# Seven products for the last feed-forward block's down-projection, the factors of gate and up exchanged, and the states' decay on GpSimd

## The chip, the cores and the metric

The kernel runs on one core of a Trainium2 chip. The metric is the device time of one execution in microseconds (us). Engines: TensorE does matmuls (PE in the profile; PEld is its weight load), VectorE (DVE) and ScalarE (ACT) work element by element and read PSUM, GpSimd (POOL) works element by element in SBUF and issues some transfers, SyncE (SP) issues the other transfers. Results of matmuls land in PSUM, eight banks of 128 x 512 fp32.

## The reference

Two layers of a streaming encoder, for 512 frames of a new stream and 8 x 16 frames of running streams: 640 rows of 1024 in all. A layer is a feed-forward block, a mixer, a feed-forward block; each is wrapped in a layer norm. So there are four feed-forward blocks, ffn0 to ffn3, of the form

```python
def swiglu(x, w_gate, w_up, w_down):
    return (jax.nn.silu(x @ w_gate) * (x @ w_up)) @ w_down
x = layer_norm(ALPHA * x + 0.5 * swiglu(x, w_gate, w_up, w_down), g, b)
```

with a hidden width of 2816 (22 rows of 128 in the kernel's layout). The first mixer is a state-space model beside stick-breaking attention, the second one a state-space mixer whose running states must be returned:

```python
h_new = h * jnp.exp(cs[:, -1])[..., None, None] + jnp.einsum('bsgr,bsgn,bsgrp->bgrpn', to_end, b_c, x_c)
```

For the 8 running streams the kernel does this last update (decay by el, plus one product) in ffn3's time, in 32 steps of 128 x 512.

## The kernel before, in words

**Precision.** All large products run in fp32r with both factors split into a high and a low part: `split` copies on ACT (the high part), then subtracts on DVE (the low part). A product is three matmuls: high x high, low x high, high x low. Weights come in as fp32 raw tiles of 128 x 1024 (four buffers, `raw`) through SP and are split into w tiles (`two_units`, six buffers) or a w1 tile (`unit`, one buffer).

**A feed-forward block.** The normed rows lie transposed as xhi and xlo (8 x 128 channels by 640 tokens). The hidden rows f = 0..21 are made in transposed form, 128 hidden channels by 640 tokens. Rows 0 and 1 and the gate of rows 2 and 3 are made with plain products (`mm3`). From row 2 on, rows are made in pairs (`pair`, f and f+1): one gate matrix and one up matrix, each a 2 x 2 block product done by seven products of blocks instead of eight (`matrix`, `product`): the weights are cut in two by hidden row and in two by input channel, x in two by channel and in two by token. Each of the seven is 12 matmuls of 320 columns. The sums of x blocks are built once per block, at the start of the stage, into the tiles T1, T2 and T4 and into x itself (`both`, earlier `minus`, and `t3_split`); the sums of weight blocks are built per matrix (`operands`) from two raw tiles. `take` is called when one of the four results is complete: for gate it applies silu, for up it multiplies by the gate, and after the last half of a hidden row `finish` splits the row into an h tile.

Four hidden rows at a time go through the down-projection, `down`, which adds into yacc (640 tokens by 1024 on five tiles of 128 tokens). It is placed between the gate and the up matrix of the next pair, so that the rows it needs are old. The last four rows (18 to 21) follow directly on the last up matrix, together with the layer norm. In the plain form it is, for each token tile t and half j, 12 matmuls of 512 columns (`tm_proj`). In the stages named in `SEVEN` the inner down-projections run as `down7`: token tile 4 stays plain, and token tiles 0 to 3 are done by seven products of blocks, with sums of hidden rows (`row_sums`, into an hs tile) and sums of weights (built in the raw tiles in place).

**PSUM.** Two pools of four banks, a and b. Gate and up use a, three banks per matrix; the plain down-projection uses b.

**Order.** The instructions of an engine are put in order by the compiler's scheduler, which takes what is ready by its own estimate, in the program's order of priority; `issue_after` adds an edge. Each engine then runs its list in order.

**The side work of ffn3.** `ssd_states` is a generator of 32 steps. `tick` advances it at given places: after a gate matrix, after an up matrix, and after token tiles 0, 2 and 4 of a down-projection. A step issues, on SP, the loads of the factors (twelve transfers every second step) and of the state; then one matmul (L1475), a multiplication by the decay (L1477, DVE), an addition of the matmul's result (L1478, DVE), and a transfer out (SP).

Lines that matter: L96 and L95 (the two halves of `split`), L141 (`mm3`), L218 (the sum into yacc in `tm_proj`), L345 (sums of weights), L366 (the matmuls of `product` in gate and up), L377 (`keep`, PSUM to SBUF on ACT), L403 and L411 (additions in gate and up), L415 and L418 (multiplications in up), L502 (the matmuls of `down7`), L510, L513 and L514 (its sums into yacc: DVE, or ACT and an accumulating transfer from POOL).

Of the kernel before, what the change touches and what calls it, by code (L numbers as in the profile page):

```python
# [9 lines left out]
F32 = mybir.dt.float32  # L10
# [11 lines left out]
T = 640  # L22
TP = 512
# [7 lines left out]
SEVEN = ("ffn1", "ffn2")  # L31
# [5 lines left out]
def kernel(ctx: ExitStack, tc: tile.TileContext, I, O, phases=PHASES):  # L37
# [28 lines left out]
    def bank_a():  # L66
        return bank("a")
# [10 lines left out]
    state = {"silu": None, "preload": None}  # L78
# [142 lines left out]
    def ffn(i, ph, last, side=None):  # L221
# [4 lines left out]
        with ExitStack() as st:  # L226
# [59 lines left out]
            g_row = lambda: wk.tile([128, T], F32, name="s", bufs=2)  # L286
            for r in range(2):
# [3 lines left out]
                for c in range(2):  # L291
                    p = bank_a()[:, :Q]
# [9 lines left out]
            def minus(t, p, m):  # L302

                u = wk.tile([128, T], F32, name="hf", bufs=2)[:, :Q]
                V.tensor_tensor(t, quad(hf32, *p)[:, k], quad(hf32, *m)[:, k], op=ALU.subtract)
                V.tensor_tensor(u, quad(lf32, *p)[:, k], quad(lf32, *m)[:, k], op=ALU.subtract)  # L306
                V.tensor_tensor(t, t, u, op=ALU.add)  # L307

            t2, t3 = (wk.tile([128, 4, Q], F32, name="h", bufs=4) for _ in range(2))
            for k in range(4):  # L310
                t1 = wk.tile([128, Q], F32, name="mx", bufs=3)
                minus(t3[:, k], (1, 1), (0, 1))
                minus(t1, (0, 1), (0, 0))
                for part in (hf32, lf32):
                    V.tensor_tensor(t2[:, k], t3[:, k] if part is hf32 else t2[:, k], quad(part, 0, 0)[:, k], op=ALU.add)  # L315
                split(tq[2][:, 0, k], tq[2][:, 1, k], t2[:, k])
                split(tq[1][:, 0, k], tq[1][:, 1, k], t1)
# [5 lines left out]
            for k in range(4):  # L323
# [3 lines left out]
            B = {1: (quad(xh, 0, 0), quad(xl, 0, 0)), 2: (quad(xh, 1, 0), quad(xl, 1, 0)),  # L327
                 3: (quad(xh, 1, 1), quad(xl, 1, 1)), 4: (tq[4][:, 0], tq[4][:, 1]), 5: (tq[1][:, 0], tq[1][:, 1]),
                 6: (tq[2][:, 0], tq[2][:, 1]), 7: (quad(xh, 0, 1), quad(xl, 0, 1))}

            def operands(src0, src1):
# [3 lines left out]
                a11, a12, a21, a22 = r0[:, :512], r0[:, 512:], r1[:, :512], r1[:, 512:]  # L335
                A = {}

                def part(w, src, *ps):
                    for n, p in enumerate(ps):
                        A[p] = w[:, n]  # L340
                    state["lo"] = split2(w, src).ins

                def total(o, v, w, op):
                    with tc.issue_after(state["lo"]):
                        V.tensor_tensor(o, v, w, op=op)  # L345
# [12 lines left out]
                A[4] = unit()  # L358
                split(A[4][:, 0], A[4][:, 1], a22)
                return A  # L360

            def product(ps, A, p, first):
                n = 0
                for k in range(4):
                    for a, b in ((0, 0), (1, 0), (0, 1)):
                        nc.tensor.matmul(ps, A[p][:, a, k * 128:k * 128 + 128], B[p][b][:, k, :],  # L366
# [3 lines left out]
            def matrix(A, take):  # L370

                x, w, z = (bank_a()[:, :Q] for _ in range(3))
                e = {}

                def keep(n, ps):
                    e[n] = wk.tile([128, Q], F32, name="mx", bufs=3)
# [1621 lines left out]
```

## Time and profile before

| | |
|---|---|
| three runs | 2546.13, 2548.44, 2544.92 us (median 2546.13) |
| profiled execution | span 2543.3 us from the first to the last instruction; no time beside the span is given for it |
| TensorE | busy 2504.3 us (98%), mean granted clock 0.997 |
| VectorE, ScalarE, GpSimd | busy 1992.5 us (78%), 1220.5 us (48%), 306.2 us (12%) |
| HBM | 259.56 MB read, 40.54 MB written |

The stages follow each other: ffn0 to about 448 us, the first mixer to 745, ffn1 to 1175, ffn2 to 1595, the second mixer to 2100, ffn3 to the end. The profile's groups give, per line and form of instruction, a count, the busy time, the mean length and the idle time before it with what ended it. In the timeline a number in brackets is such an idle time. The lengths of neighbouring rows of one engine overlap a little, and PE's far more (a matmul's row is longer than the distance to the next), so distances between starts are the better measure there.

### The profile page before, as it was taken

Reading aid. Unit: us, or ns where it says so; the run is one execution under the profiler, and the core shown is the slowest. Engines: PE = TensorE matmul, PEld = TensorE weight load, DVE = VectorE, ACT = ScalarE, POOL = GpSimd, SP = SyncE. Lnnn points to the kernel's source line nnn. Section 1 sums busy time; section 2 is a strip of 40 time slices with the busy share of each in tenths; the row PEclk is TensorE's granted clock in tenths of the full one; section 3 lists DMA queues with packets and bytes.
Section 4 is the critical chain, followed back from the end, with each engine's and each line's share of the span. In section 5 each row is a group of like instructions: output and inputs, shape, how many; then the busy total and the mean of one; then the engine's idle time right before and its main releaser. Section 6 shows DMA issues by size and latency. Waiting matters only on the chain. (4 is left out here: it accounts for less than half of the span.)

```text
span 2543.3 us, 40461 instructions
## 1 busy us (share of the span) xinstructions
PE 2504.3 (98%) x15599; PEld 2293.3 (90%) x15599; DVE 1992.5 (78%) x3437; ACT 1220.5 (48%) x2245; POOL 306.2 (12%) x432
## 2 busy tenths in 40 slices
PE   9999999999999999999999999999999999999998
PEld 9999999878789999999999999888989879999997
DVE  7788777666879888878888887777676689886768
ACT  4443444436744555553455554566565544443332
POOL 0000001210130000013000002211121151000001
PEclk9999999999999999999999999999999999999999
DMA  5322334443221433361244443456564722543442
GB/s 185 108 93 92 107 118 154 149 163 111 73 83 61 118 102 105 101 174 54 67 112 112 112 114 117 129 182 185 161 201 142 234 84 85 168 148 107 144 140 95
DMA packets 175217, 317.42 MB, mean 125 GB/s; under 512 B 20864, under 2 KB 92160, under 8 KB 174512
## 3 DMA queue, kind: packets, MB, share of 16 engines
q1 hardware_dynamic: 165200, 293.83, 36.1%
q0 software_dynamic: 9824, 21.01, 4.0%
q8 instruction: 122, 2.00, 0.3%
q14 instruction: 71, 0.58, 0.1%
HBM read 259.56 MB, written 40.54 MB: 118 GB/s over the span
## 5 line engine op out<-in xcount | busy, mean ns | idle before, releaser
L96 DVE TENSOR_TENSOR w<-raw,w 128x512 fp32r<-128x512 f32 (+2 forms) x569 | 501.2, 904 | 80.6 <-ACT w L95 79.1
L95 ACT CAST w<-raw 128x512 fp32r<-128x512 f32 (+1 forms) x569 | 425.1, 784 | 280.0 <-PE bank L141 96.7
L366 PE MATMUL bank<-xhi,w 128*128 128x320 f32 x2432 | 540.2, 309 | 0.7 <-ACT mx L377 0.5
L141 PE MATMUL bank<-xhi,w 128*128 128x256 f32 (+2 forms) x2272 | 497.7, 311 | 1.3 <-ACT xhi L205 1.0
L141 PE MATMUL bank<-w,h 128*128 128x512 f32 x1872 | 435.3, 391 | 0.4 <-DVE yacc L218 0.4
L366 PE MATMUL bank<-T,w 128*128 128x320 f32 x2736 | 426.2, 309 | 1.4 <-DVE hf L411 1.1
L141 PEld LDWEIGHTS bank<-w,h 128*128 128x128 f32 x1872 | 348.9, 188 | 73.5 <-DVE yacc L218 1.2
L366 PEld LDWEIGHTS bank<-xhi,w 128*128 128x128 f32 x2432 | 407.3, 188 | 4.8 <-ACT mx L377 1.5
L366 PEld LDWEIGHTS bank<-T,w 128*128 128x128 f32 x2736 | 406.5, 188 | 3.1 <-DVE hf L411 1.8
L141 PEld LDWEIGHTS bank<-xhi,w 128*128 128x128 f32 x2272 | 377.7, 188 | 10.8 <-issue 6.1
L366 PE MATMUL bank<-xlo,w 128*128 128x320 f32 x1216 | 375.0, 308 | 0.0
L141 PE MATMUL bank<-xlo,w 128*128 128x256 f32 (+2 forms) x1136 | 350.9, 309 | 2.6 <-DVE xlo L206 2.5
L366 PEld LDWEIGHTS bank<-xlo,w 128*128 128x128 f32 x1216 | 228.0, 188 | 0.3
L141 PEld LDWEIGHTS bank<-xlo,w 128*128 128x128 f32 x1136 | 213.9, 188 | 5.6 <-DVE xlo L206 2.8
L218 DVE SCALAR_TENSOR_TENSOR yacc<-bank,yacc 128x512 f32<-128x512 f32 x160 | 109.2, 686 | 75.3 <-PE bank L141 74.9
L377 ACT COPY mx<-bank 128x320 f32<-128x320 f32 x228 | 96.3, 423 | 138.3 <-PE bank L366 137.5
L96 DVE TENSOR_TENSOR w<-sw,w 128x1024 fp32r<-128x1024 f32 x76 | 93.0, 1224 | 52.5 <-ACT w L95 52.2
L95 ACT CAST w<-sw 128x1024 fp32r<-128x1024 f32 x76 | 79.9, 1051 | 97.2 <-DVE sw L345 96.1
L514 POOL DMA_DIRECT2D yacc<-ev x56 | 48.6, 900 | 644.5 <-ACT ev L513 589.4
L141 PE MATMUL bank<-w,og 128*128 128x512 f32 x432 | 103.7, 394 | 2.5 <-DVE og L96 1.8
L141 PEld LDWEIGHTS bank<-w,og 128*128 128x128 f32 x432 | 79.7, 188 | 19.5 <-DVE og L96 2.5
L405 ACT ACTIVATE s<-s 128x320 f32<-128x320 f32 x108 | 50.8, 470 | 82.8 <-DVE s L403 82.6
(434 smaller groups left out, 3503.8 us busy)
## 6 DMA issues: line engine op xcount, KB each, us to landing
raw<-in_w_gate_dram SPq DMA_DIRECT2D x88, 512.0 KB, 3.8
raw<-in_w_up_dram SPq DMA_DIRECT2D x88, 512.0 KB, 4.0
raw<-in_w_down_dram SPq DMA_DIRECT2D x88, 512.0 KB, 3.6
raw<-in_m_in_dram SPq DMA_DIRECT2D x52, 512.0 KB, 5.0
yacc<-ev POOLq DMA_DIRECT2D x56, 256.0 KB, 4.3
raw<-in_m_out_dram SPq DMA_DIRECT2D x24, 512.0 KB, 3.9
csb<-cs_d SPq DMA_DIRECT2D x20, 512.0 KB, 5.2
h<-in_ssd_h_dram SPq DMA_DIRECT2D x16, 512.0 KB, 6.1
```

The costliest lines, as they stand in the source:

```text
L95: nc.scalar.copy(hi, src)
L96: return nc.vector.tensor_tensor(lo, src, hi.bitcast(F32), op=ALU.subtract)
L141: state["pe"] = nc.tensor.matmul(ps, a, b, start=(k == 0), stop=(k == n - 1)).ins
L218: state["acc"] = nc.vector.scalar_tensor_tensor(ya, pb, scale, ya, op0=ALU.mult, op1=ALU.add).ins
L366: nc.tensor.matmul(ps, A[p][:, a, k * 128:k * 128 + 128], B[p][b][:, k, :], start=(first and n == 0), stop=(n == 11), skip_group_check=True)
L377: nc.scalar.copy(e[n], ps)
L405: state["silu"] = nc.scalar.activation(t, ps, AF.Silu).ins
L514: nc.gpsimd.dma_start(yacc[:, t, 512 * j:512 * j + 512], e, accum_op=ALU.add)
```

## The change

1. `SEVEN` also holds ffn3, so its four inner down-projections run as `down7`. In ffn3 the ticks after token tiles fall away for these; instead there are two in `down7`, after products 2 and 3, and the step's matmul uses a bank of pool a there.
2. In gate and up, x is the first factor of the block product and the weights the second. The order of the products is 1, 5, 6, 2, 7, 3, 4, in place of 1, 2, 6, 5, 7, 3, 4. Product 1 is copied by ACT to a second bank (z) and both copies are added to by further products; so two of the four results (up to now one) are complete in PSUM. The two z banks are a pool of their own, and the banks of a fall from four to two. The sums of the weights are built in place in the raw tiles, the sw tile goes, and the mx tile has two buffers instead of three. The last result is now the second half of row f, where before it was the second half of row f+1.
3. Tokens are taken in other halves in `down7` (tiles 0 and 1 against 2 and 3, instead of alternate tiles). One of the four row sums goes into the half of row f's h tile that is then not needed (`finish` leaves it out), so hs has 768 columns instead of 1024.
4. The multiplication by the decay in a state step goes from DVE to POOL.

The diff, cut to its core:

```diff
-SEVEN = ("ffn1", "ffn2")
+SEVEN = ("ffn1", "ffn2", "ffn3")
...
-        psum(banks[-1], f"main{len(banks)}", a=4, b=4)
+        psum(banks[-1], f"main{len(banks)}", a=2, z=2, b=4)
...
     def bank_a():
-        return bank("a")
+        if state["turn"] is None:
+            return bank("a")
+        state["turn"] += 1
+        return bank("az"[state["turn"] % 2])
...
+            sums = [bank("z")[:, :Q] for _ in range(2)]
+            state["turn"] = None
...
             for k in range(4):
-                t1 = wk.tile([128, Q], F32, name="mx", bufs=3)
-                minus(t3[:, k], (1, 1), (0, 1))
-                minus(t1, (0, 1), (0, 0))
+                t1 = wk.tile([128, Q], F32, name="mx", bufs=2)
+                both(t1, (0, 1), (1, 1), ALU.add)
+                both(t3[:, k], (0, 0), (0, 1), ALU.subtract)
...
             def operands(src0, src1):
-                u, v, w = (two_units() for _ in range(3))
-                sums = wk.tile([128, 1024], F32, name="sw", bufs=1)
-                s2, s1 = sums[:, :512], sums[:, 512:]
-                part(u, r0, 1, 2)
-                total(s1, a21, a22, ALU.add)
-                total(s2, s1, a11, ALU.subtract)
-                part(v, sums, 6, 5)
-                total(a12, a12, s2, ALU.subtract)
-                total(a11, a11, a21, ALU.subtract)
-                part(w, r0, 7, 3)
-                A[4] = unit()
-                split(A[4][:, 0], A[4][:, 1], a22)
+                split2(u, r0)
+                state["lo"] = split(v[:, 1, 0], v[:, 1, 1], b22).ins
+                total(b11, b12, b11)
+                split(v[:, 0, 0], v[:, 0, 1], b11)
+                total(b12, b22, b12)
+                total(b22, b22, b11)
+                split2(w, r1)
+                total(b21, b21, b22)
+                split(o[:, 0], o[:, 1], b21)
+                return {1: u[:, 0], 2: u[:, 1], 3: v[:, 1], 4: o, 5: v[:, 0], 6: w[:, 1], 7: w[:, 0]}
...
             def matrix(A, take):
-                x, w, z = (bank_a()[:, :Q] for _ in range(3))
+                z = sums[0]
+                sums.reverse()
+                x, w = (bank("a")[:, :Q] for _ in range(2))
...
                 product(x, A, 1, True)
-                keep(1, x)
-                product(z, A, 2, True)
-                take(0, 0, z, e[1])
-                product(x, A, 6, False)
-                keep(2, x)
+                nc.scalar.copy(z, x)
                 product(w, A, 5, True)
                 keep(5, w)
-                product(x, A, 7, False)
-                take(1, 1, x, e[5])
+                product(z, A, 6, False)
+                keep(2, z)
+                product(x, A, 2, False)
+                take(0, 0, x, None)
+                product(z, A, 7, False)
+                take(1, 1, z, e[5])
                 product(w, A, 3, False)
-                take(0, 1, w, e[2])
-                product(x, A, 4, False)
-                take(1, 0, x, None)
+                take(1, 0, w, e[2])
+                product(z, A, 4, False)
+                take(0, 1, z, None)
...
-                o = hs[f] = wk.tile([128, 2, 1024], F32R, name="hs", bufs=2)
+                o = hs[f] = wk.tile([128, 2, 768], F32R, name="hs", bufs=2)
+                split(o[:, 0, 0:512], o[:, 1, 0:512], v[0])
+                split(o[:, 0, 512:768], o[:, 1, 512:768], s4)
+                split(ht[f][:, 0, 0:256], ht[f][:, 1, 0:256], s3)
...
                     for tp in range(2):
                         product(ps[tp], tp, p, p in (1, 2, 5))
-                        add(ps[tp], 2 * tp + a, j)
+                        add(ps[tp], tp, a, j)
+                    if p in (2, 3):
+                        state["pst"] = bank_a
+                        tick(2)
+                        state["pst"] = bank_b
...
-                pst = bank_b()
+                pst = state["pst"]()
                 nc.tensor.matmul(pst, brow[:, h], xrow, start=True, stop=True)
                 h4 = h0.rearrange("p (h d) -> p h d", d=64)
-                nc.vector.tensor_tensor(h4, h4, el8[:, g, n, :, None].to_broadcast([128, 8, 64]), op=ALU.mult)
+                nc.gpsimd.tensor_tensor(h4, h4, el8[:, g, n, :, None].to_broadcast([128, 8, 64]), op=ALU.mult)
                 nc.vector.tensor_tensor(h0, h0, pst, op=ALU.add)
```

More of the change, by code (lines that the diff above doesn't have):

```diff
@@ L60, in open_banks @@
         banks.append(ExitStack())
-        psum(banks[-1], f"main{len(banks)}", a=4, b=4)
+        psum(banks[-1], f"main{len(banks)}", a=2, z=2, b=4)
+        state["turn"] = 0
     def bank(k):
@@ L76 @@
     nc.vector.memset(mhalf, -0.5)
-    state = {"silu": None, "preload": None}
+    state = {"silu": None, "preload": None, "pst": bank_b}
     def act_fn(out, in_, func, **kw):
@@ L291, in ffn @@
                 for c in range(2):
-                    p = bank_a()[:, :Q]
+                    p = bank_a()[:, :Q] if r else sums[c]
                     mm3(p, [w_k(w, k) for k in range(KT)],
@@ L334, in operands, with total @@
                 nc.sync.dma_start(r1, src1)
[L335 to L343, printed above, removed]
-                    with tc.issue_after(state["lo"]):
-                        V.tensor_tensor(o, v, w, op=op)
-                u, v, w = (two_units() for _ in range(3))
-                sums = wk.tile([128, 1024], F32, name="sw", bufs=1)
-                s2, s1 = sums[:, :512], sums[:, 512:]
-                part(u, r0, 1, 2)
-                total(s1, a21, a22, ALU.add)
-                total(s2, s1, a11, ALU.subtract)
-                part(v, sums, 6, 5)
-                total(a12, a12, s2, ALU.subtract)
-                total(a11, a11, a21, ALU.subtract)
-                part(w, r0, 7, 3)
-                A[4] = unit()
-                split(A[4][:, 0], A[4][:, 1], a22)
-                return A
+                b11, b21, b12, b22 = r0[:, :512], r0[:, 512:], r1[:, :512], r1[:, 512:]
+                u, v, w = (two_units() for _ in range(3))
+                o = unit()
+                def total(o, v, w):
+                    with tc.issue_after(state["lo"]):
+                        V.tensor_tensor(o, v, w, op=ALU.subtract)
+                split2(u, r0)
[8 more added lines that the diff above has]
+                return {1: u[:, 0], 2: u[:, 1], 3: v[:, 1], 4: o, 5: v[:, 0], 6: w[:, 1], 7: w[:, 0]}
             def product(ps, A, p, first):
@@ L365, in product @@
                     for a, b in ((0, 0), (1, 0), (0, 1)):
[L366 removed]
+                        nc.tensor.matmul(ps, A[p][:, a, k * 128:k * 128 + 128], X[p][b][:, k, :],
                                          start=(first and n == 0), stop=(n == 11), skip_group_check=True)
@@ L409, in up @@
                     t = row(f + r)
-                    if e is not None:
+                    if e is None:
+                        V.tensor_tensor(t[:, c], ps, g[r][:, c], op=ALU.mult)
+                    else:
                         V.tensor_tensor(t[:, c], ps, e, op=ALU.add)
-                        ps = t[:, c]
-                    if r == 0:
-                        if c.start:
-                            V.tensor_tensor(t, t, g[0], op=ALU.mult)
-                            finish(f)
-                    else:
-                        V.tensor_tensor(t[:, c], ps, g[1][:, c], op=ALU.mult)
-                        if not c.start:
-                            finish(f + 1)
+                        if not c.start:
+                            V.tensor_tensor(t, t, g[r], op=ALU.mult)
+                    if r == 0 and c.start:
+                        finish(f, *((256, T - 256) if seven(f) else (0, T)))
+                    elif r == 1 and not c.start:
+                        finish(f + 1)
                 for n, take in (("w_gate", gate), ("w_up", up)):
@@ L437, in pair @@
                     matrix(A, take)
-                    if n == "w_up" and ph in SEVEN and f < NF - 4:
+                    if n == "w_up" and seven(f):
                         row_sums(f)
                     tick("gate" if n == "w_gate" else "up")
-            def by_pairs(t):
-                return t[:, :TP].rearrange("p (n a c) -> p n a c", n=2, a=2)
             hs = {}
@@ L504, in product, with add @@
                             n += 1
-                def add(ps, t, j):
-                    if t // 2:
+                def add(ps, tp, a, j):
+                    t = 2 - 2 * a + tp
+                    if tp:
                         ya = yacc[:, t, j * 512:j * 512 + 512]
@@ L556, in ffn @@
                     pair(f, done if f == fs[0] else None)
+            state["turn"] = 0
             down(fs, LN_OF[ph])
@@ L929, in mixer0 @@
             banks[-1].close()
+            state["turn"] = None
             ctx_p = ExitStack()
```

41 lines of the change are left out of this document (20 added, 21 removed).

## The prediction

> **What bounds the kernel now.** I read the page's span and engine totals first.
>
> ```profile
> span 2543.3 us, 40461 instructions
> PE 2504.3 (98%) x15599; PEld 2293.3 (90%) x15599; DVE 1992.5 (78%) x3437; ACT 1220.5 (48%) x2245; POOL 306.2 (12%) x432
> ```
>
> The runs' median is 2546.13 us; the span of the one profiled execution is 2543.3 us. The 2.8 us between them lie around the span, and I carry them over unchanged. TensorE (PE) is busy 98% of the span, so only fewer or cheaper matmuls, or fewer waits of PE, can shorten it. Next, the busy times in single stretches: one period of ffn1's loop (four hid rows in, four out), from a point in one seven-product stage to the same point in the next, and the same period in ffn3. Behind the length: PE, PEld (weight loads), DVE, ACT, POOL, each with its instructions; granted clock, DMA share, GB/s.
>
> ```profile
> 1027.85:1101.88 74.03, 74.03 (x446) 69.48 (x444) 62.38 (x92) 39.15 (x59) 6.07 (x7) 1.00 0.42 110
> 2208.17:2286.25 78.08, 78.08 (x465) 73.09 (x464) 61.43 (x91) 32.16 (x52) 0.00 (x0) 1.00 0.49 158
> ```
>
> PE has no hole in either. ffn3's period is 4.05 us longer, with 19 more matmuls. What these are is seen in the chain of waits (start, length, what), which runs through PE for all of ffn3's loop:
>
> ```profile
> 2208.17 5.46 PE bank L141 x24
> 2213.63 0.23 PE bank L1475
> 2213.86 10.88 PE bank L141 x48
> 2224.74 0.23 PE bank L1475
> 2224.97 10.88 PE bank L141 x48
> 2235.84 0.23 PE bank L1475
> 2236.07 12.31 PE bank L366 x84
> ```
>
> A down-projection costs 24 + 48 + 48 = 120 matmuls of 512 columns, one per 10.88 / 48 = 0.227 us; a gate or up matrix 84 of 320 columns in 12.31 us, 1.76 us for each of its seven products; a state step one more matmul, 0.23 us. All this runs at the pace of PE; VectorE (DVE) and ScalarE (ACT) lie beneath.
>
> **Part 1: ffn3's four inner down-projections by seven products.** Each goes from 120 matmuls to 24 + 7 x 2 x 6 = 108. By the pace that is 12 x 0.227 = 2.72 us. The two periods give a smaller number, and it holds what the stage loses by itself: 4.05 us less seven state steps of 0.23 us (1.61 us) is 2.44 us. I take 2.44 x 4 = **9.8 us off**; 4 x 2.72 = 10.9 us is the other bound. The state steps are as many as before, so they cancel.
>
> What it adds to DVE, ACT and POOL is what ffn1's period already carries. ffn3 would have ffn1's 62.4 us of DVE, less four adds of 0.49 us (part 2), plus six state adds of 0.68 us: 64.5 us in a period of 78.08 - 2.44 - 0.23 = 75.4 us, 86%, against 84% in ffn1, where PE has no hole. POOL gets 7 accumulating DMAs a period, SP (the queue of the loads) no more loads than before. In the stage pool a now has two banks instead of four: its second use of a bank (product 2) starts 2.72 us (12 matmuls) after the tail's last matmul, and the add that frees it is one of 512 columns out of PSUM (0.68 us, row L1478 of part 4). Covered; uncovered it would be up to 0.68 us a stage, 2.7 us.
>
> **Part 2: x as first factor, the running sum moved on in PSUM.** It acts on all 76 matrices of 84 matmuls, whose number stays. The rows that price it (count, then busy us and mean ns):
>
> ```profile
> L403 DVE TENSOR_TENSOR s<-bank,mx 128x320 f32<-128x320 f32 x108 | 52.5, 486 | 17.3 <-PE bank L366 16.3 <-ACT w L95 0.7
> L377 ACT COPY mx<-bank 128x320 f32<-128x320 f32 x228 | 96.3, 423 | 138.3 <-PE bank L366 137.5
> L345 DVE TENSOR_TENSOR raw<-raw 128x512 f32<-128x512 f32 x76 | 52.0, 684 | 0.0
> L96 DVE TENSOR_TENSOR w<-raw,w 128x1024 fp32r<-128x1024 f32 x216 | 261.2, 1220 | 36.9 <-ACT w L95 36.3
> L366 PE MATMUL bank<-T,w 128*128 128x320 f32 x2736 | 426.2, 309 | 1.4 <-DVE hf L411 1.1 <-DVE s L403 0.2
> ```
>
> One add of 0.49 us per matrix goes (three takes add before, two after): 37 us of DVE, off the path. The three ACT copies stay three; the first goes into PSUM, which no row here shows. From below 0 (it takes the place of a copy), from above its cover: it must land within the 1.76 us of product 5 that now stands between product 1 and product 6, and the nearest row, PSUM to SBUF, takes 0.42 us. I take 0. The waits of PE inside products that exist now total 0.7 + 1.4 + 0.2 = about 2 us; DVE's relief could take these away, so the bounds are -2 and 0, and I take 0.
>
> The operands come in another order. Third now is product 6, which needs the *third* pair of splits; before, that pair served the fifth product, 3.5 us later. Behind a seven-product stage (start, length, engine):
>
> ```profile
> 1101.72 0.31 PE L366 MATMUL bank<-xhi,w 128*128 128x320 f32 x1
> 1104.17 2.35 DVE L96 TENSOR_TENSOR w<-raw,w 128x1024 fp32r<-128x1024 f32 x2
> 1106.74 1.48 PE L366 MATMUL bank<-T,w 128*128 128x320 f32 x9
> ```
>
> Even in the old order the third split's low half is done at 1105.4 (the first of the two), 1.3 us before the third product starts: no cost in the loop. The lone matmul at 1101.72, ahead of the last six of the stage, also shows that PE's order isn't the program's: what is ready is moved up while something waits. The tightest place is the first matrix of a stage, behind the building of the T tiles:
>
> ```profile
> 806.95 0.45 PE L366 MATMUL bank<-xhi,w 128*128 128x320 f32 x2
> 810.36 1.23 DVE L96 TENSOR_TENSOR w<-raw,w 128x1024 fp32r<-128x1024 f32 x1 [1.32 <-ACT w L95]
> 810.47 3.67 PE L366 MATMUL bank<-T,w 128*128 128x320 f32 x24
> 2147.61 4.44 PE L141 MATMUL bank<-w,h 128*128 128x512 f32 x18 [0.45 <-DVE yacc L218]
> ```
>
> Here the old order would end at 811.6, 1.0 us too late. The new one has on DVE before it one 1024 split, two 512 splits and three sums, against two 1024 splits, one 512 split and four sums: 1.2 us less, so it just fits. In ffn3 the T tiles come later (PE waits 0.45 us behind them), as in ffn0 with its side work. I take 0.25 us in each of these two, **0.5 us**; bounds 0 and 4 x 1.0 us. And the mx tile falls from three buffers to two, so one sum fewer can be made ahead there: one step of 320 columns (0.49 us, row L403) in the same two stages, **1.0 us**; bounds 0 and, in all four, 2.0 us.
>
> **Part 3: the last hid row of a pair is now the first (f), not the second.** In the loop it is covered by the next gate matrix. At a stage's end the last down-projection follows at once, and reads row 20 three matmuls (0.68 us) earlier than row 21. The ends of ffn3 and of ffn0:
>
> ```profile
> 2507.39 3.78 PE L141 MATMUL bank<-w,h 128*128 128x512 f32 x15
> 2508.00 1.70 DVE L96 TENSOR_TENSOR h<-hf,h 128x640 fp32r<-128x640 f32 x2
> 2509.75 1.22 PEld L141 LDWEIGHTS bank<-w,h 128*128 128x128 f32 x6 [0.33 <-DVE h L96]
> ...
> 424.32 5.79 PEld L141 LDWEIGHTS bank<-w,h 128*128 128x128 f32 x26 [0.23 <-DVE h L96]
> 424.79 0.82 DVE L96 TENSOR_TENSOR h<-hf,h 128x640 fp32r<-128x640 f32 x1
> ```
>
> PE waits here already, 0.2 to 0.3 us. In strict order that would grow by 0.68 us in four stages, 2.7 us. But in ffn0 the eleventh matmul in program order would need the low half that ends at 425.6, was due at 424.32 + 3 x 0.227 = 425.0, and no wait stands there: other matmuls were put before it. With two finished rows (18, 19) and both halves of each token block, six matmuls are free to move up. I take **0**; bounds -1.0 (today's waits gone) and +2.7 us.
>
> **Part 4: the states' decay on POOL, and fewer places for the steps.** Rows:
>
> ```profile
> L1477 DVE TENSOR_TENSOR h<-h,el 128x512 f32<-128x512 f32 x32 | 21.9, 684 | 0.8 <-DVE h L1478 0.5
> L1478 DVE TENSOR_TENSOR h<-h,bank 128x512 f32<-128x512 f32 x32 | 21.8, 680 | 8.8 <-PE bank L1475 8.8
> L1721 POOL TENSOR_TENSOR hst<-hst,el 128x512 f32<-128x512 f32 x12 | 12.9, 1072 | 74.1 <-DVE hst L1722 51.3 <-ACT hst L1719 22.7
> 2098.74 1.81 POOL L186 TENSOR_TENSOR yacc<-yacc,h 128x512 f32<-128x512 f32 x1 [1.04 <-ACT yacc L183]
> 2099.90 2.88 DVE L96 TENSOR_TENSOR w<-raw,w 128x512 fp32r<-128x512 f32 x2
> ```
>
> DVE gives up 32 x 0.68 us; POOL, idle in ffn3, does the same product in 1.07 us (the row of that shape). The decay waits only for its load, one step ahead, so the DVE add behind it shouldn't wait. The last row shows the price: two splits of 512 take 1.44 us each while POOL works, not 0.68. A decay may thus hold DVE 0.76 us, more than it saves. At 86% this stays hidden: 0.
>
> [...]
>
> Places: seven per period before, six after. The 33 steps ended before the last down-projection; now 7 + 4 x 6 = 31 do, and two fall into it. There DVE runs the norms in step with PE, so two adds of 0.68 us, less two matmuls of 0.23 us by which PE is longer there: **0.3 us**, as the first lies where DVE idles; bounds 0 and 1.4 us.
>
> **Part 5: the row sum in a hid tile.** Per pair 256 columns less are split, on ACT and DVE, under PE: 0; without that cover -0.3 us a pair.
>
> **Sum:** -9.8 + 0.5 + 1.0 + 0.3 = -8.0 us. 2546.13 - 8.0 = **2538.1 us**; the span 2535.3.
>
> **Rivals.** (A) The starts and ends take half back: PE keeps the strict order at the four ends (+2.7) and the third product waits 0.5 us in all four first matrices (+2.0 in place of 0.5): -3.8 us, 2542.3. For it: the four waits of 0.23 to 0.33 us are there already. Against it: matmuls are moved up elsewhere. (B) POOL makes DVE the bound of ffn3: a decay holds DVE when a take is due, whose cover is 1.76 us, of which the take's start and 0.49 us leave about 1.1; with a 1.22 us split in front PE waits 0.3 us for each of some 28 decays: +8.4 - 8.0, no change, 2546.5. For it the 1.44 us; against it that DVE keeps 14%. (C) Slower: the new order of operands is late in every matrix, not only the first. One wait of 0.3 us at product 6 in 76 matrices: +22.8 - 8.0, 2560.9. It decides from 8.0 / 76 = 0.11 us on. Against it stand the 1.3 us at 1105.4. (D) Better: today's waits in products and at the ends go (-2.0 and -1.0) and the starts cost nothing (-1.5): -12.5 us, 2533.6.
>
> **Chances.** Forecast 0.57 (own range 2535 to 2541), A 0.17, B 0.08, C 0.08, D 0.10. A change within 0.2% (5.1 us) can't be told from none. Faster by more: the forecast, D and a little of A, 0.70. Within: the rest of A and B, 0.22. Slower: C, 0.08. The range, 2533 to 2546, holds A and D and reaches to B; it leaves out C and half of B.
>
> **What would show it.** Right: ffn3's period 75.2 to 75.8 us with 108 down matmuls; PE without holes there; ffn0 to ffn2 as long as before within 1 us; the decay on POOL at 1.0 to 1.4 us. Wrong: waits of products for ACT's copy or for the third split, longer waits at the ends (A), DVE over 95% in ffn3 (B), or a gap at the third product in every period of ffn1 (C).

## The result, and the profile after

The changed kernel takes 2550.95 us (median of 20; 2544.47 to 2555.07) against 2545.57 us for the kernel before in the same session (median of 20): a ratio of 1.0021, 95% interval 1.0015 to 1.0027. One execution of one run below took 3049.60 us at a granted clock of 0.75 and is left out of that run's time and ratio. The forecast was 2538.1 us with a range of 2533 to 2546. The head of the page, span and engine totals:

```profile
span 2549.0 us, 40847 instructions
PE 2501.2 (98%) x15551; PEld 2289.7 (90%) x15551; DVE 2013.0 (79%) x3505; ACT 1273.8 (50%) x2389; POOL 374.5 (15%) x492
```

48 matmuls fewer and 3.1 us less PE work, and still a span 5.7 us longer: PE waits more. ffn3 starts about as early as before. These are the transposes of one token tile at ffn3's start in the timeline of PE, first in the kernel before, then in the changed one:

```profile
2103.98 1.09 PE L204 MATMUL bank<-ident,yacc 128*128 128x128 f32 x8 [0.66 <-POOL yacc L187]
```

```profile
2103.53 1.09 PE L209 MATMUL bank<-ident,yacc 128*128 128x128 f32 x8 [0.86 <-POOL yacc L192]
```

This start alone says little, since it moves between executions: in the profiles of the changed kernel and of the runs below, ffn3's first matmul of 384 columns starts between 2104.4 and 2112.8 us. The feed-forward blocks are steadier. From its first matmul of 384 columns to that of the next stage, ffn1 takes 419.8 us in all of these profiles (420.9 in the one of the kernel before) and ffn2 423.3 to 423.6 us (424.4 before). So parts 2, 3 and 5 gained about 1 us in each of the two. What moves is the rest: ffn0 takes 445.8 to 447.6 us (446.9 before), the first mixer 295.1 to 298.8, the second 500.6 to 504.9. From that matmul to the end, ffn3 takes 437.6 us, and 431.6 before: the loss is in ffn3. The stretches of its loop, from the start of one down-projection to the next, the last one up to the last down-projection (columns as in the prediction's windows):

```profile
2210.07:2285.86 75.79, 75.39 (x451) 70.58 (x450) 65.47 (x98) 39.25 (x65) 13.75 (x14) 1.00 0.56 159
2285.86:2366.67 80.81, 77.40 (x451) 71.72 (x450) 66.49 (x99) 39.37 (x66) 13.15 (x13) 0.98 0.54 150
2366.67:2444.35 77.68, 75.68 (x451) 70.55 (x450) 66.22 (x99) 40.26 (x66) 13.23 (x13) 1.00 0.55 155
2444.35:2511.08 66.73, 64.69 (x367) 59.22 (x365) 50.40 (x72) 30.92 (x52) 13.18 (x14) 0.97 0.61 170
```

The first period is what was forecast (75.2 to 75.8). The next is 5 us longer, the third 2 us, and the last stretch 4 us longer than the 62.6 us that an experiment below reaches. PE's waits in ffn3 (what for, us in total, times, longest) and the chain of waits through the last of these stages (start, length, what) say what for:

```profile
PE bank L501 <- ACT ev L513: 6.9, 3, 3.4
```

```profile
2448.04 3.84 DMA h<-in_ssd_h_dram
...
2452.05 1.24 POOL h L1483
2453.29 6.28 DMA yacc<-ev
...
2460.65 7.11 DMA yacc<-ev
...
2467.87 0.61 ACT ev L513
2468.47 0.04 issue
2468.52 4.60 PE bank L501 x12
```

This is to be read upwards. PE waits for a PSUM bank, which ACT empties into an ev tile (L513). No ev tile is free, since all three hold data of accumulating transfers that haven't landed. The second transfer couldn't start before the first had landed, as both add into the same slice of yacc (products 1 and 2). The first couldn't be issued earlier, because in POOL's list a decay (L1483) stands in front of it, and that decay waited for its state to be loaded. POOL's own rows in the second stage, two before this one:

```profile
2293.48 1.38 POOL L1483 TENSOR_TENSOR h<-h,el 128x512 f32<-128x512 f32 x1 [9.86 <-DMA h<-in_ssd_h_dram]
2294.80 0.89 POOL L514 DMA_DIRECT2D yacc<-ev  x1
2303.24 2.65 POOL L514 DMA_DIRECT2D yacc<-ev  x3 [7.55 <-ACT ev L513]
```

The first datum there had been ready 1.3 us earlier, by ACT's row:

```profile
2292.86 0.60 ACT L513 ACTIVATE ev<-bank 128x512 f32<-128x512 f32 x1 [0.17 <-PE bank L501]
```

So the late load alone did little (it landed when the datum was ready); the decay that then ran first is what the transfer waited for. PE's wait costs more than its own length. Windows over the hole of PE that follows (2308.0 to 2311.6) and over the twelve matmuls behind it:

```profile
2308.00:2311.60 3.60, 0.24 (x2) 0.00 (x0) 2.94 (x5) 1.17 (x4) 0.00 (x0) 1.00 1.09 248
2311.65:2316.26 4.61, 4.61 (x14) 3.69 (x15) 1.23 (x1) 3.26 (x5) 3.50 (x5) 0.63 0.55 149
```

The granted clock falls to 0.63 behind the hole, and twelve matmuls take 4.61 us instead of 2.73.

The groups that answer to the prediction's parts 2 and 4:

```profile
L382 ACT COPY bank<-bank 128x320 f32<-128x320 f32 x76 | 31.5, 414 | 25.6 <-PE bank L365 25.2
L1483 POOL TENSOR_TENSOR h<-h,el 128x512 f32<-128x512 f32 x32 | 42.9, 1342 | 275.3 <-DMA h<-in_ssd_h_dram 218.3 <-DVE raw L478 26.6 <-DVE s L407 20.0
```

ACT's copy inside PSUM takes 0.414 us, a little less than the copy to SBUF (0.423 in the prediction's row). The decay on POOL takes 1.34 us in the mean, within the 1.0 to 1.4 forecast.

### The profile page after: what moved, and what is told of

Same layout as the page of the kernel before. It is cut to its first block, busy times and chain, and to the rows that moved or that the text cites. A ratio compares the mean times of both kernels' runs of the same rounds, so it can differ in the third digit from the quotient of the medians.

```text
span 2549.0 us, 40847 instructions
## 1 busy us (share of the span) xinstructions
PE 2501.2 (98%) x15551; PEld 2289.7 (90%) x15551; DVE 2013.0 (79%) x3505; ACT 1273.8 (50%) x2389; POOL 374.5 (15%) x492
## 5 line engine op out<-in xcount | busy, mean ns | idle before, releaser
L101 DVE TENSOR_TENSOR w<-raw,w 128x512 fp32r<-128x512 f32 (+2 forms) x721 | 627.6, 892 | 94.9 <-ACT w L100 92.0
L100 ACT CAST w<-raw 128x512 fp32r<-128x512 f32 (+1 forms) x721 | 532.7, 769 | 324.7 <-DVE raw L348 153.0
L146 PE MATMUL bank<-w,h 128*128 128x512 f32 x1488 | 346.6, 391 | 0.0
L146 PEld LDWEIGHTS bank<-w,h 128*128 128x128 f32 x1488 | 277.4, 188 | 57.3 <-ACT h L100 1.4
L348 DVE TENSOR_TENSOR raw<-raw 128x512 f32<-128x512 f32 x304 | 210.7, 693 | 3.2
L514 POOL DMA_DIRECT2D yacc<-ev x84 | 73.6, 943 | 693.7 <-ACT ev L513 600.2
L501 PE MATMUL bank<-w,h 128*128 128x512 f32 x576 | 139.2, 396 | 6.9 <-ACT ev L513 6.9
L501 PEld LDWEIGHTS bank<-w,h 128*128 128x128 f32 x576 | 109.8, 191 | 31.2 <-ACT ev L513 8.2
L378 ACT COPY mx<-bank 128x320 f32<-128x320 f32 x152 | 64.7, 426 | 110.1 <-PE bank L365 109.5
L510 DVE SCALAR_TENSOR_TENSOR yacc<-bank,yacc 128x512 f32<-128x512 f32 x84 | 57.8, 689 | 69.3 <-PE bank L501 69.2
L223 DVE SCALAR_TENSOR_TENSOR yacc<-bank,yacc 128x512 f32<-128x512 f32 x120 | 81.8, 686 | 34.4 <-PE bank L146 33.9
L513 ACT ACTIVATE ev<-bank 128x512 f32<-128x512 f32 x84 | 50.3, 599 | 115.4 <-PE bank L501 95.1
```

Of the source, the lines that this page charges most:

```text
L100: nc.scalar.copy(hi, src)
L101: return nc.vector.tensor_tensor(lo, src, hi.bitcast(F32), op=ALU.subtract)
L146: state["pe"] = nc.tensor.matmul(ps, a, b, start=(k == 0), stop=(k == n - 1)).ins
L223: state["acc"] = nc.vector.scalar_tensor_tensor(ya, pb, scale, ya, op0=ALU.mult, op1=ALU.add).ins
L348: V.tensor_tensor(o, v, w, op=ALU.subtract)
L378: nc.scalar.copy(e[n], ps)
```

## The experiments

My first theory, T1, was that POOL's queue is at fault: decays and accumulating transfers share one list. The rivals were T2 (the transfers are slow from the steps' own loads, whoever decays), T3 (POOL's work slows DVE, which becomes the bound) and T4 (the late load stops whichever engine decays). "The version with all decays on DVE" is the first run.

### The decay back on DVE

```diff
-                nc.gpsimd.tensor_tensor(h4, h4, el8[:, g, n, ...
+                nc.vector.tensor_tensor(h4, h4, el8[:, g, n, ...
```

> The changed kernel with one line undone: the decay of the states (h times el) stands on DVE again; the steps keep their places at the second and third products of the seven-product stage. Theory T1 (POOL's queue: the decay waits for its late h load in front of the accumulating transfers, which then empty ev late): the waits of PE for ACT's ev copies (6.9 us) go and the kernel comes to 2540 to 2544. Theory T2 (the transfers are slowed by the steps' own loads and stores, whoever decays): at most 2 us are gained, 2549 or more. Theory T4 (the late h load stops whichever engine decays): the wait of 4 us per stage moves to DVE in front of the adds that empty the banks, PE waits for DVE in place of ACT, and the kernel is as slow or slower, 2550 to 2560.

Measured: 2533.85 us (2533.67 to 2539.71), ratio to the kernel before 0.9961 (0.9949 to 0.9974). This one line is 0.0060 of the time, 15 us, more than the whole loss. The same four stretches:

```profile
2205.35:2281.30 75.95, 75.52 (x451) 70.42 (x450) 69.36 (x108) 40.29 (x66) 6.04 (x7) 1.00 0.56 159
2281.30:2356.56 75.26, 75.26 (x451) 70.59 (x450) 68.20 (x105) 39.09 (x65) 6.09 (x7) 1.00 0.58 161
2356.56:2431.70 75.14, 75.14 (x451) 70.52 (x450) 68.50 (x105) 40.70 (x67) 6.08 (x7) 1.00 0.59 161
2431.70:2494.26 62.56, 62.56 (x366) 58.09 (x365) 52.19 (x77) 31.19 (x52) 7.16 (x9) 1.00 0.65 181
```

DVE is busier (91% in the periods), and PE has no hole in the last three stretches. ffn3's start in this profile, to be set beside the two rows above:

```profile
2101.14 1.09 PE L209 MATMUL bank<-ident,yacc 128*128 128x128 f32 x8 [0.84 <-POOL yacc L192]
```

It is 2.4 us earlier than in the changed kernel, and no decay has run by then. So of the 17.0 us between the two profiled spans (2549.0 and 2532.0) 2.4 lie ahead of ffn3 and say nothing on the decay; ffn3 from its first matmul of 384 columns to the end takes 423.0 us in place of 437.6, and these 14.6 us agree with the ratios. In its second stage the first transfer goes out 7.9 us after the stretch's start (8.9 in the changed kernel), and the second after 14.3 (17.4):

```profile
2289.19 0.85 POOL L514 DMA_DIRECT2D yacc<-ev  x1 [58.39 <-ACT ev L513]
2295.62 1.75 POOL L514 DMA_DIRECT2D yacc<-ev  x2 [5.58 <-DMA yacc<-ev]
```

T2 and T4 fall for these places of the steps: the h load is issued as late here (3.6 us after the start, 3.7 in the changed kernel), but DVE has other work in front of its decay. The time is 6 us below the lowest that T1 gave, so more came back than the stages' waits for ev; the slower clock behind them, for one.

### Three ways around the queue, and ffn3 left as it was

`SEVEN` without ffn3, all else changed:

> The changed kernel with ffn3 taken out of the list of seven-product stages; everything else of the change stays (x first, the sum moved in PSUM, the row sum in the hid tile, the decay on POOL, and only two places a period for the steps, so that more of the states fall behind the loop). It shows what is lost outside the seven-product stage of ffn3: if all the loss lies in that stage, chunk 0 of ffn3 takes 50.4 us as before, not 53.8, and the kernel stands near the time before plus the steps that fall late, 2546 to 2552. If part 2's new order costs chunk 0 its 3.4 us, these stay here too.

Measured 2545.64 us, ratio 1.0003 (0.9994 to 1.0012). Without ffn3's seven products the rest of the change, the decays on POOL included, comes out at nothing. ffn3's first chunk took 52.5 us in its profile, between the two lengths named.

The two ticks in `down7` taken out, a second tick behind each up matrix from row 6 on:

> The two state steps inside each seven-product stage of ffn3 are taken out and put behind up matrices of the later pairs, so no step stands in the stage; the decay stays on POOL. T1 and T2 both: the waits for ACT's ev copies go (under 1 us left), and the periods come to 75.5 us: 2539 to 2543. A theory by which the seven-product stage itself is too dense in ffn3 (its loads and accumulating transfers): the periods stay above 77 us and the kernel at 2547 or more.

Measured 2540.39 us, 0.9982 (0.9973 to 0.9991): 10 us of the 15 come back, as T1 and T2 have it.

All sums of ffn3's `down7` on DVE (`if tp or ph == "ffn3":`), so without its accumulating transfers:

> In ffn3 all sums of the seven products go into yacc on DVE (14 a stage, no accumulating transfers there, no ev tiles); the decay and the steps stay as changed. T1: POOL's wait for the h load holds nobody but the add of the state, PE's waits for ACT's ev copies are gone, 2540 to 2545. T2 likewise, since the transfers that are slow are gone. T3 (DVE is the bound in ffn3, POOL's decay slowing it): seven more adds of 0.68 us a stage make it slower than the changed kernel, 2552 or more, with DVE above 90% in the periods.

Measured 2538.60 us, 0.9977 (0.9968 to 0.9987). With the decay still on POOL 11 us come back, though DVE has seven more adds a stage. T3 as the one cause falls.

### Is it the wait for the load?

The next step's h is loaded one step earlier (`bufs=3`, the load moved ahead of the `yield`), with the decay on POOL.

> The changed kernel with the decay still on POOL, but each step's h loaded one step earlier (three h0 buffers instead of two, the load of the next step issued before the step pauses). Theory T1a (it is the wait for the late load, in POOL's queue in front of the accumulating transfers, that costs the 12 us of the four stages): POOL's waits for the h load in the stages go, PE's waits for ACT's ev copies go, and the kernel comes to 2537 to 2541 (what is lost in chunk 0 may stay). Theory T1b (it is that POOL is busy 1.0 to 1.4 us with the decay ahead of transfers, or that the transfers meet the steps' own loads): the waits for ev stay, 2546 or more.

Measured 2550.27 us, 1.0015 (1.0003 to 1.0027): nothing gained. But this doesn't decide between T1a and T1b, because the scheduler wrote the decays into POOL's list one step earlier too, and the one ahead of the transfers again stood waiting for a load:

```profile
2292.80 1.38 POOL L1492 TENSOR_TENSOR h<-h,el 128x512 f32<-128x512 f32 x1 [9.91 <-DMA h<-in_ssd_h_dram]
2294.12 0.89 POOL L514 DMA_DIRECT2D yacc<-ev  x1
```

From here on I looked at places in place of the load, and split the 32 decays between the engines by their number: `(nc.gpsimd if k in (...) else nc.vector).tensor_tensor(...)`, with k = 8g + 4 b2 + 2q + h. A ratio is good to about 0.001, a difference of two to about 0.0015, 4 us.

### Which decays cost it

Only the decay in front of each stage's first transfer on POOL (k = 8, 14, 20, 26):

> Only four of the 32 decays stay on POOL: in each seven-product stage the one that stands in POOL's queue directly in front of the stage's first accumulating transfer (the 9th, 15th, 21st and 27th); the other 28 are on DVE. Theory T1c (that one decay, waiting for its h load, starts the chain of transfers 1.1 us later, into the weight and x-row loads, and the ev tiles then come free too late): the four stages lose about what they lost in the changed kernel (11 us over 25.0 each, less what their first stage didn't lose), and the kernel comes to 2542 to 2546 though chunk 0 is not hurt. Theory T3 (POOL's work as such, 32 products of 1.0 to 1.4 us, slows DVE and with it all): four of them cost at most 4 us, 2534 to 2537.

Measured 2542.27 us (2537.62 to 2547.52), 0.9990 (0.9981 to 0.9999): four decays of 1.0 to 1.2 us cost 0.0029, 7.4 us. PE's waits for ev are back; the second stage (POOL, then PE):

```profile
2293.43 1.19 POOL L1483 TENSOR_TENSOR h<-h,el 128x512 f32<-128x512 f32 x1 [58.77 <-DMA h<-in_ssd_h_dram]
2294.57 0.88 POOL L514 DMA_DIRECT2D yacc<-ev  x1
...
2310.55 4.61 PE L501 MATMUL bank<-w,h 128*128 128x512 f32 x12 [2.53 <-ACT ev L513]
```

Could the scheduler have written another order for the rest? In the last three stretches every engine's list, by line and tile, is that of the version with all decays on DVE, but for the decay itself and one state step's matmul, which stands one matmul earlier. So what costs here is the decay on POOL and not another order. It doesn't cost in each stage: in this profile (the slowest of the eleven executions) the second and third stages wait for ev, and in the fourth, with its decay in the same place, PE doesn't wait. There the second transfer went out 4.4 us behind the first; in the second and third stages it was 7.7 and 7.3 us, and with no decay in front (the run with nine decays in the middle, below) it is 6.2 to 6.3. What sets this length is not shown.

The reverse, those four on DVE and 28 on POOL:

> The opposite: those four decays on DVE, the other 28 on POOL, one of them still among the last transfers of each stage. T1c: the stages come back to 25.0 to 25.5 us, the waits of PE for ev are gone, and only chunk 0's 2.4 us stays: 2536 to 2539. T3, or a loss through the decays behind the first transfer: 2545 or more.

Measured 2545.30 us (2537.87 to 2546.77), 1.0001 (0.9992 to 1.0010). A miss: the waits for ev are gone in the profile, but 10 us are lost all the same. The profile is of the fastest of the eleven executions, one that came to ffn3 early; its ffn3 still takes 431.8 us against 423.0 with all decays on DVE. Its waits were another kind, for DVE (4.3 us for `hf`), which the next run showed more of. Four ev tiles instead of three, the decays on POOL as changed:

> The changed kernel with four ev tiles instead of three (which hold what ACT takes from PSUM until the transfer has landed), the decays on POOL as changed. If the stage's loss is that ACT finds no free ev while transfers are late (T1c's last link), one more covers about one product, 2.7 us, of the 3 to 5 us: at least half of the 11 us comes back, 2540 to 2545. If ACT or PE wait for something else (weights not yet cast, the bank itself), nothing comes back, 2549 or more.

Measured 2546.28 us, 1.0000 (0.9992 to 1.0009): 5 us come back, and PE's waits in ffn3 are now

```profile
PE bank L365 <- DVE hf L417: 6.0, 3, 2.7
PE bank L365 <- ACT mx L378: 1.5, 1, 1.5
```

The stages are whole again (25.2, 25.0 and 25.0 us for the later three), but the first up matrix behind each waits for DVE's adds (`hf`, L417). So a second loss lay hidden behind the first. Two runs place it. The first: only the two decays around the end of each stage on POOL (k = 9, 10, 15, 16, 21, 22, 27, 28):

> POOL keeps only the eight decays that run around the end of the four seven-product stages (two per stage: one among the last two transfers, one right behind them); the other 24 are on DVE. Theory B2 (a decay on POOL stretches the DVE instructions that run at the same time, and right behind the stage DVE has a backlog of splits in front of the takes): PE waits for DVE's takes (hf) behind the stages come back, 1 to 2.7 us in three periods, and the kernel stands at 2537 to 2542 against 2533.85 with all on DVE. If those decays are harmless: 2533 to 2536.

Measured 2542.43 us (2540.65 to 2545.23), 0.9989 (0.9980 to 0.9998): 7.1 us for eight decays. Only three a period in the middle of the matrices on POOL (k = 11, 12, 13, 17, 18, 19, 23, 24, 25):

> POOL keeps only nine decays, three a period, that run in the middle of the gate and up matrices, away from the stage; the other 23 are on DVE. Theory B2: there DVE has time in hand, so nothing is lost: 2533 to 2536. If any decay on POOL costs what the mean of the 28 others seemed to cost (11.4 us / 28 = 0.4 us each): 2537 to 2538, and more if the planner's order of the loads shifts.

Measured 2533.86 us (2533.73 to 2536.82), 0.9955 (0.9943 to 0.9968): nine decays there cost nothing. The timeline of the run with the eight, at the end of its second stage (POOL, DVE, then PE):

```profile
2309.87 1.73 POOL L1483 TENSOR_TENSOR h<-h,el 128x512 f32<-128x512 f32 x1
...
2314.92 1.04 POOL L1483 TENSOR_TENSOR h<-h,el 128x512 f32<-128x512 f32 x1 [2.45 <-DMA h<-in_ssd_h_dram]
...
2310.03 2.66 DVE L101 TENSOR_TENSOR w<-raw,w 128x1024 fp32r<-128x1024 f32 x1
...
2313.21 3.29 DVE L101 TENSOR_TENSOR w<-raw,w 128x512 fp32r<-128x512 f32 x3
...
2322.89 0.48 DVE L417 TENSOR_TENSOR hf<-bank,mx 128x320 f32<-128x320 f32 x1
...
2323.42 0.56 PE L365 MATMUL bank<-xhi,w 128*128 128x320 f32 x2 [1.50 <-DVE hf L417]
```

and the same place with all decays on DVE:

```profile
2305.20 1.23 DVE L101 TENSOR_TENSOR w<-raw,w 128x1024 fp32r<-128x1024 f32 x1
...
2307.67 0.69 DVE L1483 TENSOR_TENSOR h<-h,el 128x512 f32<-128x512 f32 x1
...
2315.37 0.48 DVE L417 TENSOR_TENSOR hf<-bank,mx 128x320 f32<-128x320 f32 x1
```

A split of 1024 takes 2.66 us beside POOL's decay, 1.23 without: POOL holds DVE 1.43 us to spare it a product of 0.69; three splits of 512 beside the second decay take 3.29 us (0.69 each with DVE alone). Behind a stage DVE runs through splits and sums almost without a gap, so the add that PE waits for comes late: 11.8 us after the start of the matrix (2311.08) instead of 9.1 (after 2306.26). Not all of these 2.7 us are POOL's hold. The two decays hold DVE for 1.43 and about 1.4 us and spare it two products at 0.60 from start to start, 1.6 us net. The other 1.1 us come with the order that the scheduler then writes: one more split of 512 stands ahead of that add, and a split waits 0.39 us for ACT. What in a decay on POOL makes DVE's instruction longer is not shown; the split takes 1.43 us more beside a decay of 1.73.

### The first chunk

There are no accumulating transfers in ffn3's first chunk, yet it takes 53.8 us in the changed kernel and 51.5 with the decays on DVE (before: 50.4; no run says where this first 1 us comes from). The first eight decays on POOL, the rest on DVE:

> The decay is on POOL for the first eight steps only (up to the end of ffn3's first chunk, where no seven-product stage and no accumulating transfer runs), and on DVE for all later ones. Against the version with all decays on DVE (2533.85) it prices what POOL's decay costs in the first chunk alone: by the chunk's length (53.8 us in the changed kernel, 51.4 with the decay on DVE) I expect 2.4 us more, 2536.3, and the weight load that comes late there again. If those 2.4 us were an accident of one profile: 2533 to 2534.5.

Measured 2536.71 us, 0.9966 (0.9953 to 0.9978). Its profile has the 53.9 us, with this wait, where ACT's copy of product 1 stands behind a cast that waits for a w_down load:

```profile
2202.38 2.02 PE L365 MATMUL bank<-T,w 128*128 128x320 f32 x12 [0.90 <-ACT bank L382]
```

The kernel's time can't be told from the version with all on DVE, though (0.0005, 1.3 us, inside both intervals). Two more runs, with one decay (the seventh) and with the first four on POOL, have the scheduler's order of the loads on SP as in the changed kernel:

> POOL keeps one decay alone, the seventh, in the middle of chunk 0; the other 31 are on DVE. The order that the scheduler writes out is then the one of the changed kernel in that place: the third load of w_down stands in front of the state's rows in SP's queue, and ACT's cast of it in front of copies that PE waits for. If that order is what costs chunk 0 its 2.4 us: chunk 0 takes 53 to 54 us and the kernel 2535.5 to 2537, with PE waiting for ACT's copy into PSUM. If the eight decays cost by holding DVE: one costs 0.3 us, 2533.5 to 2534.5.

> POOL keeps the first four decays alone, which run before and in the first pair of ffn3's loop; the rest is on DVE. SP's order has the third load of w_down ahead here too, but ACT's copies stand in another order than in the changed kernel. If the order of SP's loads alone decides: 2535.5 to 2537. If POOL's overlap with DVE in the later pair of chunk 0 decides, or ACT's order: 2533.5 to 2535.

Measured 2536.73 us, 0.9967 (0.9956 to 0.9979), and 2535.39 us, 0.9965 (0.9953 to 0.9977). In their profiles the first chunk takes 51.6 and 51.5 us, so the order of SP's loads isn't the cause. ACT's order, or POOL holding DVE, is left; which, stays open.

### Places for the steps

With all decays on DVE the last down-projection still takes 37.7 us to the end (before 35.9). Three more ticks, behind the up matrices of rows 8, 12 and 16:

> All decays on DVE, and three more places for steps (behind the up matrices of the second pair of chunks 1 to 3), so that no step is left for the last down-projection. If the steps cost the last stage its 1.8 us (37.7 us from its start to the end, against 35.8 before), this gives 2532.0 with that stage back at 35.8 to 36.1; if the 1.8 us come from elsewhere, or the three steps cost as much in the loop, 2533.5 to 2535.

Measured 2537.58 us, 0.9975 (0.9965 to 0.9984). The last stage is at 35.9 us as expected, but two stages grew: the third to 26.2 us, with a wait of 0.8 us for ACT's cast of a weight, and the fourth to 27.1, with one of 1.9 us for ev. Four ev tiles with it:

> All decays on DVE, three more places for steps, and four ev tiles. With three ev tiles its last stage was 1.8 us shorter, but the third and fourth seven-product stages 1.2 and 2.1 us longer with PE waiting for ev. If the ev tiles were that loss: 2531 to 2533. If the loss is moved on to DVE's takes, as it was with the decays on POOL: 2536 to 2538.

Measured 2534.95 us (2532.64 to 2537.16), 0.9959 (0.9946 to 0.9971); the wait for ev is gone in its profile and the fourth stage is whole again, while the third is still long (25.9). So the ev tiles were a part of that loss; how much is open, as the 0.0016 between the two ratios is hardly more than their noise. Four ev tiles without the three places:

> All decays on DVE and four ev tiles. If three ev tiles still bind in some executions (the five runs with three span 2533.67 to 2539.71), the median falls to 2532 to 2533.5 and the spread shrinks. If they don't: 2533.5 to 2535, with the same spread.

Measured 2535.36 us (four executions), 0.9957 (0.9944 to 0.9971), the same as with three within the interval. Two early places instead (rows 4 and 8):

> All decays on DVE, and two more places for steps, both early (behind the up matrices of the second pairs of chunks 0 and 1), so that fewer steps fall into the last down-projection while the later stages keep the parity of their steps. If the last stage's 1.8 us go and the stages keep their 25.0 us: 2532 to 2533. If the place in chunk 0 or 1 costs as much as the tail gains, or the stages change as they did with three more places (26.2 and 27.1 us in the last two): 2534 to 2537.

Measured 2541.23 us, 0.9987 (0.9979 to 0.9996), worse than all that was expected, with a wait of 3.0 us for a DVE add into yacc and of 2.6 us for a late cast. And the steps out of the stages altogether:

> All decays on DVE, and the steps moved out of the seven-product stages to behind the up matrices (as in the run with the steps taken out), with three more places behind gate matrices so that none falls into the last down-projection. If the stages with their steps inside still lose something to the steps' loads (periods of 75.1 to 76.0 us, first 0.9 us longer), this gains up to 1 us on the version with three more places: 2531 to 2532. If POOL's queue was the whole loss, it equals that version: 2532 to 2533. If xrow's load then comes late for the second of two steps in a row, as it did once for 2.2 us with the decay on POOL: 2534 to 2536.

Measured 2551.04 us, 1.0023 (1.0013 to 1.0033), the largest miss. The last w_down load of the fourth stage stands on SP behind nine x and b rows, a store and an h load, and PE waits for ACT's cast of it:

```profile
2444.45 0.38 SPq L472 DMA_DIRECT2D raw<-in_w_down_dram  x1
```

```profile
2450.28 1.65 PE L146 MATMUL bank<-w,h 128*128 128x512 f32 x3 [5.70 <-ACT w L100]
```

So T2 is right in one thing: the steps can cost 16 us (0.0062) by their place alone, with no decay on POOL. Of PE's waits in its ffn3, 7.0 us are for ACT's casts of weights and 4.5 us for ev; how much of the rest is the loads' doing isn't shown.

## Why the prediction was wrong

**Part 1 was right.** Four times 2.44 us were to be had. With the decay on DVE the four stretches take 288.9 us; before they took 78.08, 78.12, 78.08 and 65.10, 299.4 us. That is 10.5 us. Three of the stretches hold one state step of 0.23 us fewer and the last one more, which leaves 10.0 for the 9.8 taken. The second use of a bank of pool a was covered, as said.

**Parts 2, 3 and 5.** ffn1 and ffn2 came out about 1 us shorter each, where 0 was taken, and no wait for the third split shows. One of the signs of being wrong did show, twice: a product waits for ACT's copy, 1.3 us in ffn0's first matrix and 1.0 us in ffn3's first chunk, because ACT had casts in front of it. The cover was counted from the copy's own length and not from what stands ahead of it on ACT. PE's waits inside products came to 4.9 us in all (2.1 before), a part of it through the decays. ffn0 isn't longer for it beyond its scatter. For the starts I had charged 1.5 us; from ffn3's first matmul to its first matrix it is 59.1 to 59.3 us after, 60.2 before, so they gain about 1 us.

**Part 4 failed**, with its zero for the decay. It cost 15 us by the ratios (0.0060), 14.6 in the two profiles' ffn3. Three sentences were wrong:

- "POOL, idle in ffn3", while part 1 put seven accumulating transfers a period on POOL in the same change. Each was priced alone, and the list they share was never written down.
- "The decay waits only for its load, one step ahead, so the DVE add behind it shouldn't wait". I asked who waits for the decay's result; the ones that waited stood behind it on POOL. The four decays in front of the transfers cost 7.4 us alone: one late transfer, a second one on the same slice behind it, three ev tiles, ACT, PE, and then the slower clock. That the transfers also get slower (median to landing 6.3 us in the changed kernel's ffn3, 4.9 in the run with only the first eight decays on POOL) is seen, though not in every stage; that the steps' loads do this is argued, not shown.
- "At 86% this stays hidden: 0". DVE's mean share says nothing on the stretch behind a stage, where it has no gap. The eight decays there cost 7.1 us alone, with the order that the scheduler wrote for them; nine in the middle cost none.

That 7.4 and 7.1 come near 15 is no proof that the two add up: the four decays cost 7.4 us and the 28 others 10.2, more than 15 together. In the changed kernel's own profile it is mostly the first that shows. Its four stretches are 12.1 us longer than with the decays on DVE; 6.9 of these are the waits for ev, and about 3.8 the slow matmuls behind two of them. The second appears when the first is taken away, as 6.0 us of waits with four ev tiles. The first chunk's 2.3 us in the profile are within the noise of the times. Rival B had the second mechanism, at 0.3 us for each of 28 decays and 8.4 us in all, with a chance of 0.08. The sum was close to the 7.1, the spread was not: they are few and dear. No rival had the first.

The tail's "0.3 us" was 1.8 to 2.0 (bound 1.4): 37.7 and 37.9 us from the last down-projection's start to the end, 35.9 before. Three more places brought it to 35.9, so it is the steps that fall there.

Without the one line the forecast of 2538.1 stood: 0.9961 (0.9949 to 0.9974) holds its 0.9969. That is in part luck. Part 1 was sized right, but ffn1, ffn2 and ffn3's start gained about 3 us where 1.5 were charged, and ffn3's first chunk and the tail lost 1.1 and 1.8 where 0.3 was. Four kernels with the decays on DVE, or in the middle on POOL, beat both kernels and can't be told apart (0.9955 to 0.9961). The plainest is the change with the decay left on DVE.

## What to carry to other kernels

Before an operation goes to an "idle" engine, write out that engine's list in order, transfers that it issues included, and ask of each item who stands behind it and what it waits for. Price the cover in the stretch where the operation lands, not by an engine's mean share. When one wait is removed and the time hardly moves, look for a second one that it hid, and move the suspects one group at a time. Before two profiles are compared, take the stage that the change touches by itself: here up to 8 us between two profiles lay ahead of it, most of it in the two mixers, which the change leaves alone.

## What the runs showed of the hardware

- The granted clock after a hole of PE was 0.63 in two of the changed kernel's three stages with a wait, behind idle times of 3.41 and 1.79 us, and 1.00 in the third, behind 1.72 us; it also stayed at 1.00 behind 2.75 us in the run with four ev tiles. In the run with four decays on POOL twelve matmuls took 4.61 us behind 2.53 us of idle time, as long as at the clock of 0.63 in the changed kernel (4.61 and 4.59), and 3.02 us behind 3.10, where the changed kernel's third stage takes 3.01 at 1.00. So the length of the idle time doesn't settle it; what does is not shown.
- A decay of 128 x 512 fp32 took 1.04 us on POOL in five single rows of the changed kernel's ffn3: in four DVE was busy for 0.08 to 0.49 us of that time, in the last for 0.98. It also took 1.04 beside splits of DVE that were stretched (2314.92 above). The longest took 2.48 us, with DVE busy for 2.18 of them. DVE takes 0.69 for the same product.
